# Output projection: the first eight blocks kept without x, which a chain of steps turns and adds beside the slabs

## The chip, the cores and the metric

The kernel runs on one core of a Trainium2 chip. The metric is the device time of one execution in microseconds (us), lower is better. Engines: TensorE (PE; PEld is its weight load), VectorE (DVE), ScalarE (ACT), GpSimd (POOL), SyncE (SP). DMAs are issued by instructions in the queues of SP, ACT and POOL, and an engine's queue runs in the order that was fixed when the program was built.

## The reference, cut to what matters

One layer of a decoder: 256 prompt tokens and 32 sample tokens (8 sequences of 4), D = 2048, 16 experts of which each token takes two.

```
sh1, sc1, ga1, sh2, sc2, ga2 = _adaln(c, w_ada, b_ada)
h = _rmsnorm(x, n1) * (1.0 + sc1) + sh1
...                                    # input projection, attention, gated recurrence: a, m
mix = jnp.concatenate([a, m], axis=-1) @ w_out
x = x + ga1 * mix
h2 = _rmsnorm(x, n2) * (1.0 + sc2) + sh2
x = x + ga2 * _hier_moe(h2, w_rg, b_rg, w_re, b_re, w_gate, w_up, w_down)
```

The change is in `x = x + ga1 * mix` and in the start of the second norm and of the router's logits.

## The kernel before

**Program order and the order on the engines.** The text is traced in program order; the framework then plans an order for each engine, by data dependences, by its own estimate of durations, and by program order as priority among what it holds ready. `split` (the division of a float32 tile into a rounded high part and a rest) is raised in priority. The order is fixed at build time; on the chip each engine works through its own.

**The output projection.** `out_proj` makes 32 slabs, each 512 KB of `w_out`. A slab is fetched on the ACT queue into one of three `ring0` slots (`load`, L210), split (`wh` on ACT, L495; `wl` on DVE, L496; two buffers of each), and multiplied: 24 matmuls `pf` of 128x288. Four slabs accumulate two blocks of 128 output features in two PSUM banks, and four banks (`acc`) are in use in turn, so slab n of one group of four can start only when the group before the last has had its banks emptied. Features come out transposed: a block is 128 features by 288 tokens. The order of the slabs is 0, 1, 2, 4, 5, 6, 3, 7 and then 8 to 31; below they are numbered by their place in that order, 0 to 31. Place 6 ends blocks 0 and 1, place 7 blocks 2 and 3, place 11 blocks 4 and 5, place 15 blocks 6 and 7, and so on.

**What is done with a block.** `mixed(kc, p)` empties block kc from PSUM: x (held transposed in `xT`) plus gate times product, by DVE (L1431 for the prompt, L1433 and L1434 for the samples); then the scaled copy `hA` (ACT, L1435), `hAs` (DVE), `hAb` (POOL, L1438), squares (ACT, L1440 and L1441, two buffers `sq`) and their sum `sqs` (POOL, L1443). Every fourth block turns `hA` back into rows (`pt`) and makes the router's logits (`plg`).

**The residual.** After place 6 of the slabs, the pools of the recurrence are closed and `residual` runs: four loads of `x_prompt` (512 KB each, L1464) and four of `x_sample` (64 KB each, L340) on the ACT queue into five of the seven slots of a new ring, `ring3`, which takes the closed pools' memory, and waits for the last users of it; 36 transposes `pxt` of x on PE, and nine copies into `xT`; a row shift `dsh` (matmuls `pga`) and the router's shift (`router_shift`, matmuls `prs`). Only then, in program order, comes `mixed(0)`.

**What runs beside it.** `ada` yields the steps of the modulation's matmuls: a step takes two 512 KB loads of `w_ada` (SP queue, seven slots) and makes 16 records `pm` on PE. Eight steps are woven into the last 25 slabs (`weave((out, 25), some(mods, M4))`). The experts' weights are prefetched on SP into `ring3` and `ring0`; after the projection come the second norm, the router and the experts. `tick`, called after each slab, takes the next step of a chain in `aside`; what such a step puts on PE is queued behind the slab's last matmul.

Of the kernel before, what the change touches and what calls it, by code (L numbers as in the profile page):

```python
# [10 lines left out]
F32 = mybir.dt.float32  # L11
# [3 lines left out]
AF = mybir.ActivationFunctionType  # L15
OP = mybir.AluOpType
# [4 lines left out]
KC = 16  # L21
# [96 lines left out]
def weave(*streams):  # L118

    live = [[g, n, 0] for g, n in streams if n]  # L120
    while live:
        s = min(live, key=lambda x: x[2] / x[1])
        try:
            next(s[0])
            s[2] += 1
        except StopIteration:
            live.remove(s)


class Step:  # L130
# [1287 lines left out]
        return self.run([jobs[i] for i in (0, 1, 2, 4, 5, 6, 3, 7)] + jobs[8:])  # L1418

    def mixed(self, kc, p):  # L1420
        nc = self.nc
        ga, A = self.mt[2], self.mt[4]
        cb, k = kc // 4, kc % 4
        if k == 0:
            self.hA = self.de.tile([128, 4, 256], F32, tag="hA", name="hA", bufs=2)
            self.hAs = self.de.tile([128, 4, 32], F32, tag="hAs", name="hAs", bufs=2)
            self.hAb = self.de.tile([128, 4, 128], F32, tag="hAb", name="hAb", bufs=2)
        by_seq = lambda a: a.rearrange("p (b t) -> p b t", t=4)
        bc = lambda m: m[:, kc, 1:9][:, :, None].to_broadcast([128, 8, 4])
        x, xq = self.xT[:, kc, 0:256], self.xT[:, kc, 256:288]  # L1430
        nc.vector.scalar_tensor_tensor(x, p[:, 0:256], ga[:, kc, 0:1], x, op0=OP.mult, op1=OP.add)  # L1431
        t = self.de.tile([128, 32], F32, tag="gts", name="gts", bufs=2)
        nc.vector.tensor_mul(by_seq(t), by_seq(p[:, 256:288]), bc(ga))  # L1433
        nc.vector.tensor_add(xq, xq, t)  # L1434
        nc.scalar.activation(self.hA[:, k, :], x, AF.Copy, scale=A[:, kc, 0:1])  # L1435
        nc.vector.tensor_mul(by_seq(self.hAs[:, k, :]), by_seq(xq), bc(A))
        four = lambda a: a[:, None, :].to_broadcast([128, 4, 32])
        nc.gpsimd.tensor_copy(self.hAb[:, k, :].rearrange("p (r t) -> p r t", r=4), four(self.hAs[:, k, :]))  # L1438
        sq = self.de.tile([128, 384], F32, tag="sq", name="sq2", bufs=2) if kc else self.sqs
        nc.scalar.activation(sq[:, 0:256], x, AF.Square)  # L1440
        nc.scalar.activation(sq[:, 256:384].rearrange("p (r t) -> p r t", r=4), four(xq), AF.Square)  # L1441
        if 0 < kc < KC - 1:
            nc.gpsimd.tensor_add(self.sqs, self.sqs, sq)  # L1443
        self.sql = sq
        if k == 3:
            for i in range(2):
                q = self.misc("pt2")
                for j in range(4):
                    self.tr(q[:, j * 128:(j + 1) * 128], self.hA[:, j, i * 128:(i + 1) * 128])
                self.copy(self.hs(i, cb), q)  # L1450
            q = self.misc("pt2")
            self.tr(q[:, 0:128], self.hAs.rearrange("p k t -> p (k t)"))
            self.copy(self.hs(2, cb), q[:, 0:128])
            self.logits(cb)

    def residual(self, ring):

        nc, io = self.nc, self.io
        self.xT = self.de.tile([128, KC, NT], F32, tag="xT", name="xT")
        slabs = []  # L1460
        for i in range(2):
            for h in range(2):
                t = ring[0].tile([128, 1024], F32, tag=ring[1], name="xin")
                nc.scalar.dma_start(t, io["x_prompt"][0, i * 128:(i + 1) * 128, h * 1024:(h + 1) * 1024])  # L1464
                slabs.append((i, h, t))
        t = ring[0].tile([128, 512], F32, tag=ring[1], name="xin")
        self.x_in(t.rearrange("p (k c) -> p k c", k=4), 2)
        for i, h, s in slabs:
            for q in range(2):
                p = self.misc("pxt")  # L1470
                for k in range(4):
                    self.tr(p[:, k * 128:(k + 1) * 128], s[:, (q * 4 + k) * 128:(q * 4 + k + 1) * 128])
                k0 = h * 8 + q * 4
                self.copy(self.xT[:, k0:k0 + 4, i * 128:(i + 1) * 128], p.rearrange("p (k t) -> p k t", k=4))
        p = self.misc("pxt")
        for k in range(4):
            self.tr(p[:, k * 128:(k + 1) * 128], t[:, k * 128:(k + 1) * 128])
        self.copy(self.xT[:, :, 256:288].rearrange("p (k j) t -> p k j t", j=4), p.rearrange("p (k j t) -> p k j t", k=4, j=4))

        sel = self.de.tile([128, 4, 32], F32, name="sel")  # L1480
        nc.vector.tensor_sub(sel, self.c("selb").rearrange("p (k t) -> p k t", k=4),
                             self.ident[:, 0:128:32][:, :, None].to_broadcast([128, 4, 32]))
        self.dsh = self.de.tile([128, 512], F32, name="dsh")
        p = self.misc("pga")
        for k in range(4):
            for j in range(4):
                q, c0 = self.mrow_at(k, j)
                self.mm(p[32 * j:32 * j + 32, k * 128:(k + 1) * 128], sel[:, q, :], self.mrow[3][:, c0:c0 + 128], True, True)
        self.copy(self.dsh, p)
        self.router_shift()  # L1490
        self.sqs = self.de.tile([128, 384], F32, name="sqs")
        self.lg = self.de.tile([128, 3, 20], F32, name="lg")
        self.h2 = self.mix.tile([128, 4608], F32, tag="mixT", name="h2")

    def by_rows(self):

# [15 lines left out]
    def router_shift(self):  # L1512

        p = self.misc("prs")
        for kc in range(KC):
            self.mm(p[0:9, 0:20], self.mt[3][:, kc, :], self.wr[:, kc, :], kc == 0, kc == KC - 1)
        b = self.de.tile([9, 20], F32, name="rs9")
        self.nc.vector.tensor_copy(b, p[0:9, 0:20])
        selb = self.c("selb", 9).rearrange("p (j t) -> p j t", j=4)
        p = self.misc("prs")  # L1520
        self.mm(p[:, 0:20], self.ident[0:9, 0:1].to_broadcast([9, 128]), b, True, True)
        for j in range(4):
            self.mm(p[32 * j:32 * j + 32, 32:52], selb[:, 0, :], b, True, True)
        self.rb = self.de.tile([128, 2, 20], F32, name="rb")
        for i in range(2):
            self.nc.vector.tensor_add(self.rb[:, i, :], p[:, 32 * i:32 * i + 20], self.br)

    def logits(self, cb):

        nc = self.nc  # L1530
        pl = self.misc("plg")
        for i in range(3):
            for k in range(4):
                l = self.hA[:, k, i * 128:(i + 1) * 128] if i < 2 else self.hAb[:, k, :]
                self.mm(pl[:, i * 20:(i + 1) * 20], l, self.wr[:, cb * 4 + k, :], k == 0, k == 3)
        lg = self.lg.rearrange("p i e -> p (i e)")
        if cb == 0:
            nc.vector.tensor_copy(lg, pl[:, 0:60])
        else:
            nc.vector.tensor_add(lg, lg, pl[:, 0:60])  # L1540
# [140 lines left out]
    def turned(self, sa):  # L1681
        p = self.misc("pht")
        for k in range(4):
            self.tr(p[:, k * 128:(k + 1) * 128], sa[:, k * 128:(k + 1) * 128])
        hT = self.ex.tile([128, 4, 128], F32, tag="hidT", name="hidT", bufs=2)
        self.copy(hT.rearrange("p k s -> p (k s)"), p)
        return hT
# [195 lines left out]
def body(tc, nc, io, stop=None):  # L1883
    s = Step(tc, io)
# [3 lines left out]
    def pool(name, side="left", bufs=1, space=None):  # L1888
        more = {"space": space} if space else {"side": side, "reuse_waits": "tile"}
        return tc.tile_pool(name=name, bufs=bufs, **more)  # L1890

    def some(gen, n):
        return islice(gen, n), n

    with pool("const") as const, pool("ring0", bufs=R0) as r0, pool("ring1", bufs=R1) as r1, \
# [48 lines left out]
        with pool("keep") as s.keep, pool("hga") as s.hga, pool("cc") as s.cc:  # L1944
# [8 lines left out]
            with pool("hg") as s.hg:  # L1953
# [4 lines left out]
                out = s.out_proj()  # L1958
# [9 lines left out]
        with pool("de") as s.de, pool("ring3", bufs=R3) as r3:  # L1968
            s.residual((r3, "w3"))
            weave((out, 25), some(mods, M4))  # L1970
            s.use("out", exp=[(r3, "w3")] * R3 + [r0] * R0)
            s.fetching, s.ahead = s.fetches(), []
            s.look_ahead(R3 + R0)
            held.close()
            with pool("ex", "right") as s.ex:
                s.norm2()
                s.route()
                for _ in mods:
                    pass
                s.use("experts", exp=[r1] * R1 + [r2] * R2 + [(r3, "w3")] * R3 + [r0] * R0)  # L1980
                s.once = [(s.ex, "x")] * 4 if XR else []
                s.look_ahead(R3 + len(rings) + len(s.once))
                s.experts()
# [24 lines left out]
```

## Time and profile before

| | |
|---|---|
| time, median of 3 runs | 1470.29 us (1467.14 to 1472.81) |
| the profiled execution's time | 1465.81 us |
| its span (first to last instruction) | 1463.9 us |
| PE busy | 1356.1 us (93%) |
| DMA | 457.25 MB, mean 312 GB/s |
| output projection's last 25 slabs, residual included | about 772 to 892 us of the span |

Times in rows are us from the span's start. In a timeline a row is: start, duration, engine, line, operation, out<-in, shape, count, and in brackets the idle time before it with what ended it. ACTq, SPq are DMA issues in the queues of ACT and SP. The matmuls overlap, so a run of n of them takes less than n times the duration of one.

### The profile page before, as it was taken

To read this page: it belongs to the slowest core of one execution; us is meant where nothing else is said; L and a number is where in the kernel's file an instruction comes from. 1 tells how busy PE (TensorE), PEld (TensorE's weight loads), DVE (VectorE), ACT (ScalarE), POOL (GpSimd) and SP (SyncE) were. 2 spreads that over 40 slices of the span, in tenths; PEclk is the share of its full clock that TensorE was granted. 3 is DMA by queue.
4 is the path that set the end of the run, shared out by engine and by line. 5 is a ranking of instruction groups with operands and counts; after the bars stand their busy time and mean duration, and the time that the engine had idled before them with its cause. 6 is when DMAs were issued, how large, how long until landed. Compare 5 with 4: busy or idle time off the path is not lost. (4 is left out here: it accounts for less than half of the span.)

```text
span 1463.9 us, 30058 instructions
## 1 busy us (share of the span) xinstructions
PE 1356.1 (93%) x11808; PEld 925.8 (63%) x11808; DVE 650.9 (44%) x1571; ACT 368.3 (25%) x687; POOL 145.7 (10%) x178
## 2 busy tenths in 40 slices
PE   4889899989999997999998999999999999699997
PEld 3566677777888885788775997563535445253532
DVE  2332355565885454796453444123234141413134
ACT  3222233455443353343332442010000000000000
POOL 2000201010001010012011222001010010101011
PEclk9999999999999998999998998899999999799999
DMA  9999998648889987889979646769999999799997
GB/s 314 368 382 328 354 339 306 232 152 264 287 268 290 287 271 236 274 268 309 329 235 345 243 159 238 297 268 366 399 389 396 395 388 398 269 398 387 398 387 283
DMA packets 240807, 457.25 MB, mean 312 GB/s; under 512 B 17178, under 2 KB 84619, under 8 KB 240395
## 3 DMA queue, kind: packets, MB, share of 16 engines
q1 hardware_dynamic: 171218, 374.60, 71.1%
q10 hardware_dynamic: 66818, 74.10, 15.1%
q0 software_dynamic: 2624, 6.56, 1.3%
q8 instruction: 95, 1.56, 0.4%
q14 instruction: 52, 0.43, 0.1%
HBM read 446.94 MB, written 8.26 MB: 311 GB/s over the span
## 5 line engine op out<-in xcount | busy, mean ns | idle before, releaser
L496 DVE TENSOR_TENSOR wl<-w,wh 128x1024 fp32r<-128x1024 f32 x128 | 159.5, 1246 | 164.2 <-ACT wh L495 159.8
L148 PE MATMUL pf<-hhi,wh 128*128 128x288 f32 x640 | 200.4, 313 | 1.7 <-ACT lf L788 1.4
L495 ACT CAST wh<-w 128x1024 fp32r<-128x1024 f32 x128 | 133.9, 1046 | 269.4 <-PE pf L148 199.8
L148 PE MATMUL pf<-hlo,wh 128*128 128x288 f32 x640 | 193.9, 303 | 0.0
L148 PE MATMUL pf<-hhi,wl 128*128 128x288 f32 x640 | 193.5, 302 | 0.0
L148 PE MATMUL pm<-w,cT 128*32 128x128 f32 (+1 forms) x2048 | 126.7, 361 | 26.9 <-DMA w<-w_ada 26.2
L148 PEld LDWEIGHTS pf<-hhi,wh 128*128 128x128 f32 x640 | 122.2, 191 | 17.6 <-issue 14.2
L148 PE MATMUL pa<-w,hp 128*64 128x512 f32 x512 | 118.3, 618 | 8.1 <-DMA w<-w_exp_up 8.1
L148 PEld LDWEIGHTS pf<-hlo,wh 128*128 128x128 f32 x640 | 122.6, 192 | 4.1 <-issue 3.8
L148 PEld LDWEIGHTS pf<-hhi,wl 128*128 128x128 f32 x640 | 122.5, 191 | 2.1 <-issue 1.9
L148 PE MATMUL pu<-w,hp 128*64 128x512 f32 x512 | 116.1, 594 | 0.5 <-DMA w<-w_exp_up 0.5
L148 PE MATMUL py<-w,hidT 128*64 128x512 f32 x512 | 114.6, 602 | 0.8 <-DVE hidT L196 0.8
L148 PEld LDWEIGHTS pm<-w,cT 128*32 128x32 f32 x2048 | 61.8, 118 | 71.0 <-DMA w<-w_ada 35.9
L148 PEld LDWEIGHTS pg<-oh,h 128*128 128x128 f32 x768 | 89.4, 196 | 6.5 <-issue 6.5
L148 PE MATMUL pg<-oh,h 128*128 128x128 f32 x768 | 91.5, 281 | 0.0
L148 PEld LDWEIGHTS pa<-w,hp 128*64 128x64 f32 x512 | 37.1, 143 | 80.5 <-issue 74.4
L1402 POOL TENSOR_TENSOR x<-x,gt 128x512 f32<-128x512 f32 x24 | 33.2, 1382 | 524.0 <-DVE gt L1400 521.6
L148 PEld LDWEIGHTS pu<-w,hp 128*64 128x64 f32 x512 | 37.9, 137 | 74.6 <-issue 68.4
L1679 DVE SCALAR_TENSOR_TENSOR sa<-sa,cs,pu 128x512 f32<-128x512 f32 x8 | 6.0, 747 | 172.8 <-PE pu L148 172.8
L148 PEld LDWEIGHTS py<-w,hidT 128*64 128x64 f32 x512 | 36.9, 138 | 72.0 <-issue 64.3
L148 PE MATMUL pf<-mhi,wh 128*128 128x288 f32 x256 | 77.5, 304 | 0.2 <-ACT mhi L495 0.2
L148 PE MATMUL pf<-mlo,wh 128*128 128x288 f32 x256 | 76.9, 301 | 0.0
(427 smaller groups left out, 2004.2 us busy)
## 6 DMA issues: line engine op xcount, KB each, us to landing
w<-w_ada SPq DMA_DIRECT2D x192, 512.0 KB, 7.2
w<-w_exp_gate SPq DMA_DIRECT2D x128, 512.0 KB, 10.6
w<-w_exp_up SPq DMA_DIRECT2D x128, 512.0 KB, 9.7
w<-w_exp_down SPq DMA_DIRECT2D x128, 512.0 KB, 10.5
w<-w_in ACTq DMA_DIRECT2D x96, 512.0 KB, 5.4
w<-cache_k SPq DMA_DIRECT2D x128, 256.0 KB, 4.3
w<-cache_v SPq DMA_DIRECT2D x128, 256.0 KB, 4.4
w<-w_out ACTq DMA_DIRECT2D x32, 512.0 KB, 3.6
```

Source lines behind the costliest of these rows:

```text
L148: return self.queued(self.nc.tensor.matmul(out, lhsT=lhsT, rhs=rhs, start=start, stop=stop))
L495: self.nc.scalar.copy(hi, x)
L496: self.nc.vector.tensor_sub(lo, x, hi.bitcast(F32))
L1402: eng.tensor_add(x, x, t[:, 0:n])
L1679: self.nc.vector.scalar_tensor_tensor(sa, sa, cs, pu, op0=OP.mult, op1=OP.mult)
```

## The change

For the first eight blocks `mixed` no longer reads x: ACT writes gate times product of the prompt into `xT`, and DVE that of the samples. `residual` still issues the loads of x at the same place (in the order of column halves), but all the rest of it becomes a chain, `joined`, whose steps are taken one after each slab from place 7 on: `sel`, `dsh`, the router's shift in two steps, then x for blocks 0 to 3 (transposed on PE, added to `xT` by DVE from PSUM), `scaled(0..3)`, x for blocks 8 to 15 (copied into `xT` as before), the rows and logits of blocks 0 to 3 (`block(0)`, in two steps), x for blocks 4 to 7 with `scaled(4..7)`, and `block(1)`. The blocks from 8 on are added to x as before, and `block(2)` becomes a chain too. In the diff, the unchanged middle of `scaled`, the bodies of `block` and the new signature of `logits` are left out, as are the chain's first four steps (`sel`; `pga` and `dsh`; the router's shift in two).

```diff
@@ mixed @@
-        cb, k = kc // 4, kc % 4
+        x, xq = self.xT[:, kc, 0:256], self.xT[:, kc, 256:288]
+        if kc < 8:
+            nc.scalar.activation(x, p[:, 0:256], AF.Copy, scale=ga[:, kc, 0:1])
+            nc.vector.tensor_mul(by_seq(xq), by_seq(p[:, 256:288]), gs)
+            return
+        nc.vector.scalar_tensor_tensor(x, p[:, 0:256], ga[:, kc, 0:1], x, op0=OP.mult, op1=OP.add)
+        t = self.de.tile([128, 32], F32, tag="gts", name="gts", bufs=2)
+        nc.vector.tensor_mul(by_seq(t), by_seq(p[:, 256:288]), gs)
+        nc.vector.tensor_add(xq, xq, t)
+        self.scaled(kc)
+        if kc % 4 == 3:
+            steps = self.block(kc // 4)
+            if kc < KC - 1:
+                self.aside[0].append(steps)
+            else:
+                for _ in steps:
+                    pass
+
+    def scaled(self, kc):
...
+    def block(self, cb):
+        hA, hAs, hAb = self.hA, self.hAs, self.hAb
...
+        yield
+        self.logits(cb, hA, hAb)
 
     def residual(self, ring):
...
-        for i in range(2):
-            for h in range(2):
+        for h in range(2):
+            for i in range(2):
                 t = ring[0].tile([128, 1024], F32, tag=ring[1], name="xin")
                 nc.scalar.dma_start(t, io["x_prompt"][0, i * 128:(i + 1) * 128, h * 1024:(h + 1) * 1024])
                 slabs.append((i, h, t))
         t = ring[0].tile([128, 512], F32, tag=ring[1], name="xin")
         self.x_in(t.rearrange("p (k c) -> p k c", k=4), 2)
...
+        self.aside[0].append(self.joined(slabs, t))
+
+    def joined(self, slabs, sample):
+        nc = self.nc
+        plus = lambda out, p: nc.vector.tensor_add(out, out, p)
+        def turned(i, h, s, q):
+            p = self.misc("pxt")
+            for k in range(4):
+                self.tr(p[:, k * 128:(k + 1) * 128], s[:, (q * 4 + k) * 128:(q * 4 + k + 1) * 128])
+            k0 = h * 8 + q * 4
+            (self.copy if h else plus)(self.xT[:, k0:k0 + 4, i * 128:(i + 1) * 128], p.rearrange("p (k t) -> p k t", k=4))
+        def sampled(*ks):
...
+        yield
...
+        for x in slabs[0:2]:
+            turned(*x, 0)
+        sampled(0)
+        yield
+        for k in range(4):
+            self.scaled(k)
+        yield
+        turned(*slabs[2], 0)
+        turned(*slabs[3], 0)
+        yield
+        turned(*slabs[2], 1)
+        turned(*slabs[3], 1)
+        sampled(2, 3)
+        yield
+        yield from self.block(0)
+        yield
+        for x in slabs[0:2]:
+            turned(*x, 1)
+        sampled(1)
+        for k in range(4, 8):
+            self.scaled(k)
+        yield
+        yield from self.block(1)
@@ body @@
             s.residual((r3, "w3"))
             weave((out, 25), some(mods, M4))
+            s.finish_aside()
```

## Rows read from the trace of the kernel before

**Rows 1.** Busy time of each engine in four stretches: from the cast of the slab at place 9 to the first matmul of place 8, then two stretches of the projection, and one of the experts. Columns: stretch, length, busy us and instructions of PE, PEld, DVE, ACT and POOL, granted clock, DMA share, GB/s.

```profile
776.00:800.20 24.20, 17.31 (x198) 10.00 (x197) 6.00 (x13) 4.64 (x9) 0.14 (x1) 0.79 0.95 351
808.00:840.00 32.00, 32.00 (x247) 31.87 (x246) 15.83 (x27) 13.95 (x23) 7.79 (x8) 1.00 0.65 226
840.00:892.00 52.00, 52.00 (x409) 50.14 (x409) 24.62 (x45) 20.85 (x35) 12.16 (x14) 1.00 0.57 189
988.00:1100.00 112.00, 107.89 (x641) 47.51 (x636) 35.59 (x63) 5.88 (x10) 8.34 (x6) 0.98 1.03 385
```

**Rows 2.** The same view for two stretches of 5 us inside the first of them.

```profile
780.00:785.00 5.00, 1.62 (x10) 0.55 (x10) 0.00 (x0) 0.00 (x0) 0.00 (x0) 0.62 1.03 417
790.00:795.00 5.00, 4.75 (x34) 2.61 (x38) 0.69 (x1) 1.66 (x3) 0.00 (x0) 0.66 0.89 275
```

**Rows 3.** Groups of PE's matmuls by operation from 776 to 800.2 us: count | busy us, mean ns of one | idle before them and what ended it.

```profile
L148 PE MATMUL pm<-w,cT 128*32 128x256 f32 x96 | 9.6, 463 | 4.4 <-DMA w<-w_ada 4.2
L152 PE MATMUL pxt<-cst,xin 128*128 128x128 f32 x36 | 6.3, 329 | 2.5 <-DMA xin<-x_prompt 2.1 <-DMA xin<-x_sample 0.5
```

**Rows 4.** Timeline of PE and DVE from 767 us to the first matmul of place 8 at 800.17.

```profile
766.97 1.93 PE L148 MATMUL pm<-w,cT 128*32 128x256 f32 x32
...
783.38 1.92 PE L148 MATMUL pm<-w,cT 128*32 128x256 f32 x10 [4.21 <-DMA w<-w_ada]
...
790.25 1.10 PE L152 MATMUL pxt<-cst,xin 128*128 128x128 f32 x8 [2.09 <-DMA xin<-x_prompt]
...
795.84 1.09 PE L152 MATMUL pxt<-cst,xin 128*128 128x128 f32 x8
...
797.74 0.47 DVE L1431 SCALAR_TENSOR_TENSOR xT<-pf,mt,xT 128x256 f32<-128x256 f32 x1
...
798.38 1.08 PE L148 MATMUL pga<-mrow,sel 128*32 128x128 f32 x32
...
799.28 0.96 PE L148 MATMUL prs<-wr,mt 128*9 128x20 f32 x32
...
800.17 0.40 PE L148 MATMUL pf<-mhi,wh 128*128 128x288 f32 x1
```

**Rows 5.** Timeline of the stores of the recurrent state on POOL, and of ACT and its DMA issues around the loads of x; one row of DVE (the split's second half).

```profile
774.25 1.49 POOL L1068 DMA_DIRECT2D new_state_sample<-st  x2 [3.58 <-DVE st L1064]
...
776.00 1.05 ACT L495 CAST wh<-w 128x1024 fp32r<-128x1024 f32 x1 [5.45 <-PE pf L148]
776.01 0.35 ACTq L1464 DMA_DIRECT2D xin<-x_prompt  x1
...
777.08 1.23 DVE L496 TENSOR_TENSOR wl<-w,wh 128x1024 fp32r<-128x1024 f32 x1 [3.38 <-ACT wh L495]
...
781.90 1.36 ACTq L1464 DMA_DIRECT2D xin<-x_prompt  x3
784.21 0.60 ACTq L340 DMA_DIRECT2D xin<-x_sample  x1
790.22 1.88 ACTq L340 DMA_DIRECT2D xin<-x_sample  x3
...
792.14 1.07 ACT L194 COPY xT<-pxt 128x512 f32<-128x512 f32 x2 [15.09 <-DMA xin<-x_prompt]
...
794.25 0.39 ACTq L210 DMA_DIRECT2D w<-w_out  x1
```

**Rows 6.** DMA issues from 775 to 800 us: tile, queue, count, KB each, median us from issue to landing.

```profile
xin<-x_prompt ACTq DMA_DIRECT2D x4, 512.0 KB, 10.4
...
new_state_sample<-st POOLq DMA_DIRECT2D x2, 256.0 KB, 6.4
w<-w_out ACTq DMA_DIRECT2D x1, 512.0 KB, 5.4
```

**Rows 7.** Waits of SP's DMA queue from 740 to 960 us: the waiting issue <- what it waited for: us in total, times, longest.

```profile
SPq L210 <- DMA xin<-x_prompt: 10.1, 2, 7.5
```

**Rows 8.** Timeline of ACT: the casts of `w_out` after the gap; the first two of 22.

```profile
808.00 1.05 ACT L495 CAST wh<-w 128x1024 fp32r<-128x1024 f32 x1 [3.56 <-PE pf L148]
...
811.19 1.05 ACT L495 CAST wh<-w 128x1024 fp32r<-128x1024 f32 x1 [2.15 <-PE pf L148]
```

**Rows 9.** Instructions on the tile `xT`: count, duration in ns (minimum, median, maximum), first and last start.

```profile
L1431 DVE SCALAR_TENSOR_TENSOR xT<-pf,mt,xT x16: 474/480/486, 797.7 to 891.9; 128x256 f32<-128x256 f32 x16
L1435 ACT ACTIVATE hA<-xT,mt x16: 492/500/512, 798.7 to 892.4; 128x256 f32<-128x256 f32 x16
...
L196 DVE COPY xT<-pxt x5: 681/691/692, 786.4 to 798.5; 128x512 f32<-128x512 f32 x5
```

**Rows 10.** Timeline of POOL in the projection: the same two operations alone, and beside DVE's splits.

```profile
800.06 0.29 POOL L1438 COPY hAb<-hAs 128x128 f32<-128x128 f32 x1 [24.32 <-DVE hAs L1436]
...
801.31 1.00 POOL L1443 TENSOR_TENSOR sqs<-sqs,sq 128x384 f32<-128x384 f32 x1 [0.17 <-ACT sq L1441]
...
819.94 1.78 POOL L1443 TENSOR_TENSOR sqs<-sqs,sq 128x384 f32<-128x384 f32 x1 [1.15 <-ACT sq L1441]
822.07 1.23 POOL L1438 COPY hAb<-hAs 128x128 f32<-128x128 f32 x1 [0.34 <-DVE hAs L1436]
```

**Rows 11.** Timeline of SP's DMA queue after the gap.

```profile
797.06 7.07 SPq L1718 DMA_DIRECT2D w<-w_exp_gate  x7
805.02 66.61 SPq L210 DMA_DIRECT2D w<-w_ada  x5
```

More of the change, by code (lines that the diff above doesn't have):

```diff
@@ L1421, in mixed @@
         nc = self.nc
-        ga, A = self.mt[2], self.mt[4]
-        cb, k = kc // 4, kc % 4
+        ga = self.mt[2]
+        by_seq = lambda a: a.rearrange("p (b t) -> p b t", t=4)
+        gs = ga[:, kc, 1:9][:, :, None].to_broadcast([128, 8, 4])
+        x, xq = self.xT[:, kc, 0:256], self.xT[:, kc, 256:288]
[17 more added lines that the diff above has]
+        nc = self.nc
+        A = self.mt[4]
+        k = kc % 4
         if k == 0:
@@ L1428, in mixed @@
         by_seq = lambda a: a.rearrange("p (b t) -> p b t", t=4)
-        bc = lambda m: m[:, kc, 1:9][:, :, None].to_broadcast([128, 8, 4])
         x, xq = self.xT[:, kc, 0:256], self.xT[:, kc, 256:288]
[L1431 to L1434, printed above, removed]
         nc.scalar.activation(self.hA[:, k, :], x, AF.Copy, scale=A[:, kc, 0:1])
-        nc.vector.tensor_mul(by_seq(self.hAs[:, k, :]), by_seq(xq), bc(A))
+        nc.vector.tensor_mul(by_seq(self.hAs[:, k, :]), by_seq(xq), A[:, kc, 1:9][:, :, None].to_broadcast([128, 8, 4]))
         four = lambda a: a[:, None, :].to_broadcast([128, 4, 32])
@@ L1444, in mixed @@
         self.sql = sq
-        if k == 3:
-            for i in range(2):
[L1447 to L1450, printed above, removed]
-            q = self.misc("pt2")
-            self.tr(q[:, 0:128], self.hAs.rearrange("p k t -> p (k t)"))
-            self.copy(self.hs(2, cb), q[:, 0:128])
-            self.logits(cb)
+    def block(self, cb):
+        hA, hAs, hAb = self.hA, self.hAs, self.hAb
+        for i in range(2):
+            q = self.misc("pt2")
+            for j in range(4):
+                self.tr(q[:, j * 128:(j + 1) * 128], hA[:, j, i * 128:(i + 1) * 128])
+            self.copy(self.hs(i, cb), q)
+        q = self.misc("pt2")
+        self.tr(q[:, 0:128], hAs.rearrange("p k t -> p (k t)"))
+        self.copy(self.hs(2, cb), q[:, 0:128])
+        yield
+        self.logits(cb, hA, hAb)
     def residual(self, ring):
@@ L1460, in residual @@
         slabs = []
-        for i in range(2):
-            for h in range(2):
+        for h in range(2):
+            for i in range(2):
                 t = ring[0].tile([128, 1024], F32, tag=ring[1], name="xin")
@@ L1467, in residual @@
         self.x_in(t.rearrange("p (k c) -> p k c", k=4), 2)
[L1468 to L1478, printed above, removed]
+        self.sqs = self.de.tile([128, 384], F32, name="sqs")
+        self.lg = self.de.tile([128, 3, 20], F32, name="lg")
+        self.h2 = self.mix.tile([128, 4608], F32, tag="mixT", name="h2")
+        self.aside[0].append(self.joined(slabs, t))
+    def joined(self, slabs, sample):
+        nc = self.nc
+        plus = lambda out, p: nc.vector.tensor_add(out, out, p)
[6 more added lines that the diff above has]
+        def sampled(*ks):
+            p = self.misc("pxt")
+            for k in ks:
+                self.tr(p[:, k * 128:(k + 1) * 128], sample[:, k * 128:(k + 1) * 128])
+                (plus if k < 2 else self.copy)(self.xT[:, 4 * k:4 * k + 4, 256:288],
+                                               p[:, k * 128:(k + 1) * 128].rearrange("p (j t) -> p j t", j=4))
+        yield
         sel = self.de.tile([128, 4, 32], F32, name="sel")
@@ L1489, in residual @@
         self.copy(self.dsh, p)
[L1490 to L1493, printed above, removed]
+        yield
+        yield from self.router_shift()
+        yield
[12 more added lines that the diff above has]
+        sampled(2, 3)
+        yield
+        yield from self.block(0)
+        yield
+        for x in slabs[0:2]:
[3 more added lines that the diff above has]
+            self.scaled(k)
+        yield
+        yield from self.block(1)
     def by_rows(self):
@@ L1518, in router_shift @@
         self.nc.vector.tensor_copy(b, p[0:9, 0:20])
+        yield
         selb = self.c("selb", 9).rearrange("p (j t) -> p j t", j=4)
@@ L1526, in router_shift, with logits @@
             self.nc.vector.tensor_add(self.rb[:, i, :], p[:, 32 * i:32 * i + 20], self.br)
-    def logits(self, cb):
+    def logits(self, cb, hA, hAb):
         nc = self.nc
@@ L1533, in logits @@
             for k in range(4):
-                l = self.hA[:, k, i * 128:(i + 1) * 128] if i < 2 else self.hAb[:, k, :]
+                l = hA[:, k, i * 128:(i + 1) * 128] if i < 2 else hAb[:, k, :]
                 self.mm(pl[:, i * 20:(i + 1) * 20], l, self.wr[:, cb * 4 + k, :], k == 0, k == 3)
```

## The prediction

> **What bounds the kernel now.** I read the busy time by stretches first [rows 1]. In the experts DMA is full (1.03, 385 GB/s) with PE at 96%, and from 808 to 892 us PE is busy without a gap while DMA stands at 0.57 to 0.65. Between 776.0 and 800.2 it is otherwise: PE is busy 17.3 of 24.2 us, and part of that at a granted clock of 0.62 to 0.66, a mean over the two levels of 1.2 and 2.4 GHz, after waits of several us [rows 2]. So this stretch holds lost PE time, and what follows it is PE-bound until 892. The experts begin from whatever time that leaves: their loads are paced by slots that PE frees, and DMA had room before. A gain there should reach the end whole.
>
> What PE needed there I make from the groups [rows 3] and from what the same work takes in runs at full clock [rows 4]: 96 records of `pm` at 1.93/32 = 0.060 us, 5.8; 36 transposes at 1.09/8 = 0.136, 4.9; `pga` 1.1; `prs` 1.0. Together 12.8 of 24.2 us, so 11.4 us are lost.
>
> Why PE waits: place 8 starts at 800.17, behind the first emptying of a block, DVE's 797.74 [rows 4]. Its split had long been made; what lacks is a bank, since `mixed(0)` adds to an x that is only being loaded and turned. And x is late for two reasons. The second to fourth loads of `x_prompt` are issued at 781.90, about when the last stores of the state land (774.25 plus 6.4) [rows 5, 6], whose memory `ring3` takes over; three of the `x_sample` loads only at 790.22 [rows 5]. The code gives the last ones no reason, but SP's issues of `w_ada` too are held by landings of x [rows 7], so an issue can wait for an earlier DMA of the other queue. While ACT's queue holds an issue, the engine holds everything behind it: there is no ACT work between 777.05 and 792.1 and no `w_out` load before 794.25 [rows 5].
>
> **The change part by part.**
>
> *Emptying without x.* Blocks 0 to 3 need only their products and the gate. ACT takes about 0.5 us for a 128x256 with a scale, DVE 0.48 for what it replaces [rows 9]. Blocks 0 and 1 are complete before place 7, so they should be emptied before the x loads become ready, and place 8 should follow place 7 at about 776 or one `pm` step (16 records, 0.96) later. ACT's added 8 x 0.5 us lie in 116 us where it is busy 40% [rows 1]: nothing on the path.
>
> *The chain.* PE gets the same 36 transposes, `pga`, `prs`, `pt` and `plg`, only later, between slabs; the 12.8 us are moved, not saved. DVE adds 128x512 from PSUM where DVE or ACT copied: no row shows that add; bounded by the copy, 0.69, and by twice that [rows 9]; I take 0.7. Four such adds, 3 to 6 us, lie in DVE's idle half [rows 1].
>
> *What stays.* The eight x issues stand at the same place in ACT's queue, with the same waits. So the cast for place 10, ready when place 8 is done, can be caught behind them. A slab costs 3.19 us (808.00 to 811.19) [rows 8]. PE from 776.0: one `pm` step, places 8 and 9, `pga`: 1.0 + 6.4 + 1.1, to 784.5. ACT: the three x loads end at 783.3, the sample's four take 0.6 each [rows 5]. If they are held only by the first x load (784.2), they end at 786.6, and cast and `wl` take 2.3 more (776.00 to 778.31) [rows 5]: place 10 at 788.9, a stall of 4.4. If the planner puts the cast ahead of them, 785.6, a stall of 1.1. I take 3. If they are held until 790.22 as now, ACT is free at 792.1 and place 10 starts at 794.4: a stall of 10.
>
> *The next in line* is the `w_out` slab of place 12, issued behind x at about 786.6. Its landing: 5.4 us as now, or 10.4 as x's in the full queue [rows 6], so 792 to 797, plus 2.3. PE reaches place 12 after places 10 and 11 (6.4), a `pm` step and `prs` (2.0), from 787.5: at 795.9. The stall is 0 to 3.4; I take 1. DMA has less to do there than before: `pm` steps are no longer run in a row, and their slots ask for `w_ada` later.
>
> *The sum.* 11.4 lost now; 3 + 1 lost after; gain 7.4 us. The profiled execution of 1465.81 (span 1463.9) would become 1458.4. It stands 4.5 us under the median of the runs shown, 1470.29, from which I take the same 7.4: 1462.9. A measurement of this kernel tells about 0.5%, 7.4 us, so the forecast stands on that line.
>
> Costs that I put at nothing: five `ring3` slots stay with x until place 18 instead of 798, so up to five expert loads move back by some 40 us; DMA at 0.57 to 0.65 hides them [rows 1]; without that cover they would be 5 x 0.5 MB at 385 GB/s, 6.8 us. [...]
>
> **The rivals.**
>
> *All of the stall goes.* If the emptying, the cast and the load for place 12 all come ahead of the x loads in the planned order, or the waits fall differently, nothing is left in the stretch: 11.4 us, 1458.9. For it: the cast of place 9 came ahead of the x loads, though its text stands behind them [rows 5]. Against it: place 10's cast is ready 3 to 4 us later, and the x issues then are not yet through.
>
> *The stall moves from x's landing to x's issue.* ACT is held until 792.1: 11.4 - 10 = 1.4 us of gain, 1468.9. For it: the issues at 790.22 as they are [rows 5]. Against it: the hold goes by which DMAs were issued between, and five of the `w_ada` loads around them should move away with their `pm` steps. The Trainium skill, "DMA: Bandwidth & Descriptors", section "Anatomy of one DMA", says that a DMA's semaphore wait happens on the issuing sequencer before dispatch; this trace agrees, with 15 us without ACT work.
>
> *Bursts of `scaled`.* Four blocks' `scaled` come in one step, twice. POOL takes 0.29 + 1.00 for a block alone, 1.23 + 1.78 beside other work [rows 10], 3.0 against ACT's 1.2. With two `sq` buffers ACT's third square would wait for POOL's sum, and a cast stand behind it. Of each burst two squares wait 1.8 us, and so do those that pile up: 4 to 11 us of ACT in all, of which the 0.9 us of slack in a slab of 3.19 (2.3 used) covers a part. The gain shrinks to 4, or to a loss of 3.6: 1466 to 1474. Against it: casts are raised in priority, ACT and POOL are mostly idle, and pairs of blocks stretched in the same way cost PE nothing from 808 on [rows 1, 10]. The Trainium skill, "SBUF — State Buffer", section "Who interferes with whom", states as a rule that a DVE instruction with two SBUF inputs contends with a GpSimd one that reads SBUF; the split's second half is such an instruction, and the stretched 1.23 and 1.78 agree.
>
> *Slower: SP's queue.* The expert loads for slots that x holds could stand in SP's order ahead of `w_ada` loads, as seven of them do now [rows 11]. The slots come free after place 18, at about 797 + 7 x 3.2 = 819; the seven `w_ada` slots hold three and a half steps, so that from the fifth step, about place 16 to 19 (810), PE would wait until 819 plus a landing of about 7: some 16 us. Then 1462.9 + 16 = 1479. It decides as soon as one such load stands ahead of the fifth step's; the planner takes what it holds ready first, which speaks against it.
>
> **How the numbers follow.** Forecast (gain 5 to 9.5 us, 1460.8 to 1465.3) 0.43; all of the stall gone (1458 to 1460.8) 0.20; the stall moved (1465.3 to 1470) 0.19; bursts (1466 to 1474) 0.10; SP's queue (1477 to 1481) 0.08. Under 1462.9 lie the second case and a bit more than half of the first: faster 0.45. Over 1477.6 lie most of the last and a little for what I do not see: slower 0.10. The same 0.45. The range leaves out most of the last two and a little below: 1457 to 1470.5; the forecast's own is 1460.8 to 1465.3.
>
> **What the profile after would show.** Right: `pf` of place 8 at 776 to 778, not 800; ACT's scaled copies ahead of the x issues; a first PE gap near 784 that a cast ends, not DMA x; a second, if any, ended by `w_out`; `pxt` from about 800 on, between slabs, without gaps; the projection's last `pf` and everything behind it 5 to 10 us earlier, with the experts' stretch as long as now. Wrong would be: the x issues held until 792 with PE idle from 784; casts idle for `sq`; SP holding an expert load before a late `w_ada`; or an earlier end of the projection that the experts take back.

## The result, and the profile after

The changed kernel takes 1459.92 us (median of 12 runs, 1457.46 to 1468.62) against 1469.47 (12 runs, 1463.48 to 1474.22) for the kernel before. The medians are 9.6 us apart; the ratio taken over the runs is 0.9946, with a 95% interval of 0.9925 to 0.9968, and by it the change is worth 8 us, 5 to 11 by the interval. The forecast was 1462.9. The profiled execution took 1457.83 us, with a span of 1455.8.

First the busy time of each engine by stretches of the kernel after, from the end of place 7 to the end of the projection (columns as in [rows 1]):

```profile
771.00:788.20 17.20, 17.20 (x194) 15.35 (x193) 4.54 (x6) 3.43 (x4) 0.00 (x0) 1.00 1.01 372
788.20:803.00 14.80, 11.77 (x97) 9.99 (x98) 6.12 (x14) 5.91 (x10) 0.94 (x4) 1.00 0.85 286
803.00:835.00 32.00, 30.98 (x256) 29.00 (x255) 16.51 (x31) 17.06 (x39) 9.76 (x14) 1.00 0.73 247
835.00:843.00 8.00, 8.00 (x55) 8.00 (x54) 1.35 (x2) 2.14 (x5) 2.35 (x3) 0.79 0.60 200
843.00:882.00 39.00, 39.00 (x322) 36.89 (x321) 16.32 (x31) 14.60 (x26) 8.06 (x9) 1.00 0.65 213
```

Where PE was busy 17.31 of 24.2 us, with a granted clock of 0.79 [rows 1], it now works 17.2 us without a gap at 1.00, and DMA is as full as it was. The gap is not gone: 3.0 us of it are found in 788.2 to 803. PE's timeline says at which matmuls:

```profile
770.94 1.07 PE L148 MATMUL pm<-w,cT 128*32 128x256 f32 x16
771.94 0.40 PE L148 MATMUL pf<-mhi,wh 128*128 128x288 f32 x1
...
791.09 0.40 PE L148 MATMUL pf<-mhi,wh 128*128 128x288 f32 x1 [1.42 <-ACT wh L495]
...
800.37 0.40 PE L148 MATMUL pf<-mhi,wh 128*128 128x288 f32 x1 [0.89 <-ACT wh L495]
...
801.63 0.40 PE L148 MATMUL pf<-mhi,wl 128*128 128x288 f32 x1 [0.72 <-DVE wl L496]
```

Place 8 starts at 771.94, one `pm` step after place 7, where it stood 24 us behind it [rows 4]. Places 9 to 11 follow without a gap. The gaps that are left stand at places 12 and 14, and both wait for a cast. ACT's timeline tells why the casts are late (under it, three of its DMA issues by themselves):

```profile
760.98 0.83 ACT L1428 ACTIVATE xT<-pf,mt 128x256 f32<-128x256 f32 x2
...
771.06 0.35 ACTq L1488 DMA_DIRECT2D xin<-x_prompt  x1
771.87 0.47 ACT L1428 ACTIVATE xT<-pf,mt 128x256 f32<-128x256 f32 x1
776.27 0.35 ACTq L1488 DMA_DIRECT2D xin<-x_prompt  x1
776.66 1.05 ACT L495 CAST wh<-w 128x1024 fp32r<-128x1024 f32 x1 [4.33 <-DMA new_state_sample<-st]
776.84 0.82 ACTq L1488 DMA_DIRECT2D xin<-x_prompt  x2
778.51 1.05 ACT L495 CAST wh<-w 128x1024 fp32r<-128x1024 f32 x1 [0.80 <-PE pf L148]
778.52 5.08 ACTq L340 DMA_DIRECT2D xin<-x_sample  x4
784.91 3.75 ACTq L210 DMA_DIRECT2D w<-w_out  x2
788.71 0.47 ACT L1428 ACTIVATE xT<-pf,mt 128x256 f32<-128x256 f32 x1 [9.15 <-DMA w<-w_out]
789.99 1.04 ACT L495 CAST wh<-w 128x1024 fp32r<-128x1024 f32 x1 [0.81 <-DMA w<-w_out]
...
799.27 1.04 ACT L495 CAST wh<-w 128x1024 fp32r<-128x1024 f32 x1 [4.37 <-DMA w<-w_out]
```

```profile
783.03 0.57 ACTq L340 DMA_DIRECT2D xin<-x_sample  x1
784.91 0.40 ACTq L210 DMA_DIRECT2D w<-w_out  x1
788.27 0.39 ACTq L210 DMA_DIRECT2D w<-w_out  x1
```

Blocks 0 and 1 are emptied at 760.98, ahead of every load of x. The cast for place 10 (776.66) was planned between the second and the third x load, and the one for place 11 ahead of the `x_sample` loads. Then ACT's queue is held at DMA issues. A row of several issues spans the waits between them: of the 5.08 us of `x_sample` the issues themselves are 2.9 (2.48 before: 0.60 and 1.88 [rows 5]), and ahead of the fourth, at 783.03, the queue waits 2.1 us. It waits 1.3 us more before `w_out` for place 12 goes out at 784.91, and 3.0 us before the next `w_out`, at 788.27. From place 12 on the casts wait for `w_out` to land.

The trace tells what these issues wait for: each waits for a semaphore (a counter that a landing DMA raises), and an earlier DMA carries the same one. The fourth `x_sample` load shares its semaphore with the second `x_prompt` load, which lands at 783.00; `w_out` for place 12 shares one with the third `x_prompt` load, which lands at 784.89. In all four profiles of the changed kernel these two are the same, and this `w_out` is issued 0.02 us after that landing.

SP's queue shows what else the full DMA carries in that time:

```profile
762.59 9.88 SPq L210 DMA_DIRECT2D w<-w_ada  x6
775.01 3.68 SPq L1782 DMA_DIRECT2D w<-w_exp_gate  x2
787.64 5.18 SPq L210 DMA_DIRECT2D w<-w_ada  x4
```

Two loads of the experts' weights, the first of which stood at 797.06 before [rows 11], are issued at 775 and 778, into the two slots of `ring3` that x leaves free.

**How much of the 8 us is the change.** Each kernel has four profiled executions. The table cuts the span in four. PE idle is length less busy time in one window over the stretch from the end of place 7 to the projection's last matmul; lost to clock is half of PE's busy time in those spells of the stretch in which the granted clock was 0.50.

| profile | time | place 7 ends | stretch behind it | of it PE idle | lost to clock | norm, router | experts |
|---|---|---|---|---|---|---|---|
| before, 1 | 1465.81 | 776.1 | 115.8 | 6.9 | 4.0 | 41.2 | 530.8 |
| before, 2 | 1468.64 | 779.4 | 115.4 | 6.8 | 3.4 | 41.1 | 530.9 |
| before, 3 | 1470.0 | 777.0 | 118.0 | 8.2 | 5.0 | 41.3 | 531.8 |
| before, 4 | 1471.96 | 782.0 | 117.2 | 8.3 | 3.9 | 39.7 | 531.0 |
| **mean** | 1469.1 | 778.6 | 116.6 | 7.5 | 4.1 | 40.8 | 531.1 |
| after, 1 | 1457.83 | 771.0 | 111.0 | 4.1 | 1.7 | 39.4 | 534.4 |
| after, 2 | 1460.12 | 773.8 | 112.4 | 4.6 | 2.6 | 41.2 | 530.9 |
| after, 3 | 1466.04 | 781.8 | 110.5 | 2.4 | 3.4 | 39.3 | 531.9 |
| after, 4 | 1462.9 | 776.5 | 109.0 | 2.4 | 1.7 | 43.9 | 531.8 |
| **mean** | 1461.7 | 775.8 | 110.7 | 3.4 | 2.3 | 41.0 | 532.3 |

The stretch of the change is 5.9 us shorter: 4.2 less idle and 1.7 less lost to the clock. Length less both losses is 105 us within 0.3 in every row: the work is the same. Of the 7.4 us between the means, 2.9 come from ahead of place 7's end and 1.2 are given back behind the stretch; both are smaller than the spread between profiles of one kernel. PE's instructions ahead of there are the same; ACT and DVE empty blocks 0 to 2 in the last 10 us of it, but in the first pair of profiles the kernels are 5.1 us apart before that (the same DVE row at 754.65 and at 749.56).

### The profile page after: what moved, and what is told of

It reads as the page before. It is cut to its first block, busy times and chain, and to the rows that moved or that the text cites. A ratio compares the mean times of both kernels' runs of the same rounds, so it can differ in the third digit from the quotient of the medians.

```text
span 1455.8 us, 30060 instructions
## 1 busy us (share of the span) xinstructions
PE 1351.4 (93%) x11808; PEld 923.0 (63%) x11808; DVE 645.6 (44%) x1559; ACT 370.0 (25%) x694; POOL 142.9 (10%) x178
## 5 line engine op out<-in xcount | busy, mean ns | idle before, releaser
L148 PE MATMUL pm<-w,cT 128*32 128x128 f32 (+1 forms) x2048 | 122.2, 355 | 19.6 <-DMA w<-w_ada 19.1
L148 PEld LDWEIGHTS pf<-hhi,wh 128*128 128x128 f32 x640 | 121.3, 190 | 17.2 <-issue 13.8
L148 PE MATMUL pf<-mhi,wl 128*128 128x288 f32 x256 | 76.8, 300 | 0.7 <-DVE wl L496 0.7
## 6 DMA issues: line engine op xcount, KB each, us to landing
w<-w_exp_gate SPq DMA_DIRECT2D x128, 512.0 KB, 10.5
w<-w_exp_down SPq DMA_DIRECT2D x128, 512.0 KB, 10.5
```

The source lines that it names most:

```text
L148: return self.queued(self.nc.tensor.matmul(out, lhsT=lhsT, rhs=rhs, start=start, stop=stop))
```

## The experiments

**The two kernels again.** First beside the experiments below:

> The kernel before, profiled once more. In the two profiles at hand the first matmul of place 7 starts at 771.8 (before) and 766.7 us (after), though all that runs up to there is the same program; the stretch from the end of place 7 to the end of the projection's last slab matmul takes 115.8 and 111.0 us. Theory (the 5.1 us ahead of the change are chance, the change's own part is the stretch): the stretch is again 115.8 within 0.7, and the start of place 7 lies anywhere from 765 to 774. Rival (the 5.1 us belong to the change, by its code's place or size): the start is again 771.8 within 1 us.

> The changed kernel, profiled once more. Theory: the stretch from the end of place 7 to the last slab matmul is again 111.0 us within 0.7, with a first gap of 1 to 2 us at place 12 that a late w_out load ends, and the start of place 7 lies anywhere from 765 to 774. Rival (the time ahead belongs to the change): it starts at 766.7 within 1 us.

> The kernel before, profiled a third time. Theory (ahead of place 7 is chance, the change's own part in the projection is about 4 us): the stretch from the end of place 7 to the last slab matmul is again 115.4 to 115.8 us, gaps of 10 to 11.5 us in it; the start of place 7 anywhere from 765 to 777. Rival (the kernel before is slower ahead of place 7 for a reason of its own): the start lies later than 771 again, and later than in the changed kernels of this call.

Then, since the changed kernel had been early ahead of place 7 already in both of its profiles:

> A further look at the changed kernel as it is. Three looks at the kernel before ended place 7 at 776.1, 779.4 and 777.0 us, two at the changed one at 771.0 and 773.8, though no engine's instructions differ ahead of there. If that is chance, place 7 ends anywhere from 771 to 779 here; if the change moves it, at 771 to 774. The stretch from there to the projection's last matmul: 111 to 112.5 us if the two looks so far are typical, and any difference between looks is made of spells at the lower clock and of the gap at place 12.

> The same again, on the same terms: place 7 ends at 771 to 774 if the change moves it, anywhere from 771 to 779 if it is chance; the stretch behind it 110 to 113 us.

> A fourth look at the kernel before, on the same chip as these: place 7 ends at 776 to 780 if the two kernels differ ahead of there, anywhere from 771 to 779 if it is chance; the stretch behind it 115 to 118 us, about 4.5 more than the changed kernel's.

Measured: the table above. Place 7 of the changed kernel ended at 781.8 and 776.5 in its last two profiles, of the kernel before at 782.0: the ranges lie over each other, 771 to 782 and 776 to 782. The five variants below, which are the same up to there but for one wait, ended it at 772.0 to 777.9. So the 5 us by which the first profile was ahead there can't be told from chance, and the first pair of profiles alone would have told a wrong story, a gain of 8 us of which the change's own stretch held 4.8. The stretch, 109.0 to 112.4 against 115.4 to 118.0, doesn't overlap. It spreads more than was expected: of the six repeats two, the first and the last of the kernel before, fall where the stretch was put; 112.4, 110.5 and 109.0 of the changed kernel and 118.0 of the kernel before miss by 0.5 to 2.2 us. The ends of place 7 at 781.8 and 782.0 lie outside what either theory gave, 771 to 780.

**Undone: blocks 0 and 1 wait for x, all else as changed.** The emptying gets a bias that is x times zero, from the last `x_prompt` load.

```diff
-            nc.scalar.activation(x, p[:, 0:256], AF.Copy, scale=ga[:, kc, 0:1])
+            if kc < 2:
+                nc.scalar.activation(x, p[:, 0:256], AF.Identity, bias=self.zero, scale=ga[:, kc, 0:1])
+            else:
+                nc.scalar.activation(x, p[:, 0:256], AF.Copy, scale=ga[:, kc, 0:1])
@@ residual, behind the loads @@
+        self.zero = self.de.tile([128, 1], F32, name="zero")
+        nc.gpsimd.tensor_scalar(self.zero, slabs[3][2][:, 0:1], 0.0, None, op0=OP.mult)
```

> The changed kernel, but the emptying of blocks 0 and 1 waits for the landing of the last of the four x_prompt loads (its bias is that slab's first column times zero); the chain and all its steps stay. Theory (the gain is that the banks are emptied before x is there): place 8 starts at about 788 to 792 instead of 772, minus what pm and pga can fill, the stretch grows by 9 to 14 us to 120 to 125, and the kernel is no faster than before: ratio 0.998 to 1.005. Rival (the gain is that the transposes and the rest are spread between slabs): the ratio stays at 0.995 and the stretch at 111.

Measured: 1474.16 us, ratio 1.0039 (1.0018 to 1.0061), as expected; the stretch is 126.2 us, 1.2 above the range given (in a profiled execution of 1478.41 us). ACT's timeline, and under it the first matmul of place 8 in PE's:

```profile
784.60 1.36 ACTq L1491 DMA_DIRECT2D xin<-x_prompt  x3
787.08 7.55 ACTq L340 DMA_DIRECT2D xin<-x_sample  x4
798.70 0.56 ACT L1429 ACTIVATE xT<-pf,zero,mt 128x256 f32<-128x256 f32 x1 [19.73 <-DMA xin<-x_sample]
```

```profile
799.54 0.61 PE L148 MATMUL pf<-mhi,wh 128*128 128x288 f32 x1 [2.50 <-DVE xT L1432]
```

With the wait for x back, place 8 is back at 799.54, 21.9 us behind place 7 (17 to 21 were expected), with ACT idle for 19.7 us behind the issues of x. The whole gain hangs on the emptying that doesn't wait for x; the chain by itself gains nothing, nor does the new order of the x loads or ACT in DVE's place, which this variant keeps. That the stretch is 9.6 us longer than the mean before fits the order: the turning of x, which filled 4.9 us of the gap before, now comes after it. PE is idle for 13.9 us of the stretch against 7.5, and loses 8.3 us to the lower clock against 4.1.

**Expert loads held back, 1.** No load of the experts' weights is issued before the last `w_ada` load.

```diff
+        d = getattr(self.nc, QUEUE[kind]).dma_start(dst, src)
+        if kind == "ada":
+            self.last_ada = d.ins
@@ body @@
-            s.look_ahead(R3 + R0)
+            with tc.issue_after(s.last_ada):
+                s.look_ahead(R3 + R0)
```

> The changed kernel, but the first ten expert loads stand on SP behind the last w_ada load of the projection; in the changed kernel two of them (1 MB) are issued at 775 and 778 us, ahead of the w_out loads that PE then waits for at places 12 to 14 (3.5 us in three gaps). Theory A (those gaps are a full DMA): the two loads are 2.6 us at 400 GB/s, the gaps shrink by 1.5 to 2.6 us and the stretch to 108.5 to 109.5. Theory B (the gaps are the late issue of w_out behind x on ACT's queue): the stretch stays at 111 within 0.5. For either: the experts start no later, since DMA has room from 846 on; if it has not, the gap shows as a wait of the first expert.

Measured: 1461.39 us, ratio 0.9952 (0.9927 to 0.9978). The busy time in two windows, SP's queue, ACT's issue of `w_out` for place 12, and PE's wait in the second window:

```profile
777.70:802.00 24.30, 24.16 (x255) 20.73 (x255) 7.29 (x12) 6.34 (x8) 0.00 (x0) 1.00 1.01 344
840.00:860.00 20.00, 17.93 (x134) 16.88 (x133) 6.79 (x13) 5.87 (x11) 3.39 (x5) 0.91 0.96 343
```

```profile
834.82 7.97 SPq L1784 DMA_DIRECT2D w<-w_exp_gate  x7
```

```profile
789.21 2.75 ACTq L210 DMA_DIRECT2D w<-w_out  x2
```

```profile
850.15 0.40 PE L148 MATMUL pf<-mhi,wh 128*128 128x288 f32 x1 [1.34 <-ACT wh L497]
```

The gaps at places 12 and 14 are gone: so the two early expert loads made them. How they did can be read from the issues. `w_out` for place 12 now shares its semaphore with a `w_ada` load issued 10 us before, and goes out 11.5 us behind place 7 (at 789.21), as soon as the `x_sample` issues are through; in the changed kernel it is 13.9 to 15.9. It isn't that DMA has room: the third `x_prompt` load lands 13.8 us behind place 7, against 13.9 to 15.9, and from its issue to its cast `w_out` takes 6.4 us, against 4.8 to 6.1.

But now seven expert loads go out in a row at 834.82, DMA is full there, and the casts wait for `w_out` at place 23: PE idles 2.1 us in that window, 2.6 in the stretch. Here the landing itself is late: that `w_out`, issued at 839.02, is cast at 849.05. The stretch is 109.9 us, between the 108.5 to 109.5 of the one theory and the 110.5 to 111.5 of the other.

**Expert loads held back, 2.** The same, but they may go from an earlier `w_ada` load on (`ada_loads` lists these in order), so that they don't come in one row.

```diff
-            s.look_ahead(R3 + R0)
+            with tc.issue_after(s.ada_loads[171]):
+                s.look_ahead(R3 + R0)
```

> The changed kernel, but its ten first expert loads stand on SP behind one earlier w_ada load (that of the sixth of the eight steps, issued at about 792 in the changed kernel), so that the two that were issued at 775 and 778 follow the w_out loads of places 12 to 14, and the others stay spread. Theory A (the left-over gaps are the full DMA): no gap at places 12 to 14 and none near 850, where seven expert loads in a row delayed w_out when they were all held to 835; gaps of 1 to 2 us in all, stretch 107.5 to 109; the kernel 2 to 4 us faster than the changed one, ratio 0.990 to 0.994. Rival (what the projection gains is taken back by the router's stretch and the experts): stretch as said, but a ratio of 0.995 and a first expert matmul that starts no earlier after the residual's place than in the changed kernel.

Measured: 1460.82 us, ratio 0.9940 (0.9918 to 0.9961). ACT's timeline, and two windows:

```profile
786.19 2.62 ACTq L342 DMA_DIRECT2D xin<-x_sample  x4
788.86 1.86 ACTq L210 DMA_DIRECT2D w<-w_out  x2
...
794.82 1.04 ACT L497 CAST wh<-w 128x1024 fp32r<-128x1024 f32 x1 [0.95 <-DMA w<-w_out]
```

```profile
777.80:803.00 25.20, 25.20 (x265) 22.10 (x266) 9.57 (x15) 8.02 (x11) 0.00 (x0) 1.00 1.04 354
...
825.80:829.80 4.00, 4.00 (x21) 4.00 (x20) 1.06 (x1) 0.00 (x0) 0.00 (x0) 0.57 0.48 162
```

PE has no gap in 25.2 us behind place 7 (777.8), though DMA is still full, 1.04. What has changed is the time in ACT's queue: `x_sample` goes out in 2.62 us without a wait (5.1 to 5.8, waits included, in the four profiles of the changed kernel), `w_out` for place 12 is issued 11.1 us behind place 7 (13.9 to 15.9 there) and its cast runs 17.0 us behind it (19.0 to 22.0), 6.0 us after the issue. As in the variant before, its semaphore is that of a `w_ada` load and not of the third `x_prompt` load. PE's idle time in the stretch is 1.5 us against 3.4. By its runs the kernel is not told apart from the changed one, where 2 to 4 us were expected: two spells of lower clock, one of them in the window at 0.57, cost 3.4 us of the stretch, which takes 109.3 (107.5 to 109 expected).

**x loads put off.** The `x_sample` loads are issued in the chain's third step, the second halves of `x_prompt` in its fourth, to bring `w_out` for place 12 forward.

```diff
-                nc.scalar.dma_start(t, io["x_prompt"][0, i * 128:(i + 1) * 128, h * 1024:(h + 1) * 1024])
+                if h == 0:
+                    self.load_x(i, h, t)
...
-        self.x_in(t.rearrange("p (k c) -> p k c", k=4), 2)
@@ joined @@
+        self.x_in(sample.rearrange("p (k c) -> p k c", k=4), 2)
...
+        for x in slabs[2:4]:
+            self.load_x(*x)
```

> The changed kernel, but the sample's loads are issued with the chain's third step and the two x_prompt loads of the second column half with its fourth; w_out of place 12 then stands ahead of 1 MB of x on ACT's queue, w_out of place 13 behind it. The two early expert loads stay. Theory A (full DMA): as 1 MB less stands ahead of it, w_out of place 12 lands 2 to 3 us earlier and its gap of 1.5 to 3.5 us goes, that of places 13 and 14 stays or grows to 2 or 3: stretch 109 to 111, ratio 0.993 to 0.996. Theory B (issue order alone): all gaps at places 12 to 14 go, stretch 107 to 108.

Measured: 1465.91 us, ratio 0.9949 (0.9925 to 0.9973); its runs spread from 1455.5 to 1467.9, so that median and ratio don't say quite the same. ACT's timeline and PE's:

```profile
787.56 0.60 ACTq L210 DMA_DIRECT2D w<-w_out  x1
788.20 1.00 ACTq L1482 DMA_DIRECT2D xin<-x_prompt  x2
791.95 1.05 ACT L495 CAST wh<-w 128x1024 fp32r<-128x1024 f32 x1 [3.98 <-DMA w<-w_out]
791.97 0.42 ACTq L210 DMA_DIRECT2D w<-w_out  x1
...
803.26 1.04 ACT L495 CAST wh<-w 128x1024 fp32r<-128x1024 f32 x1 [7.42 <-DMA w<-w_out]
```

```profile
804.35 0.61 PE L148 MATMUL pf<-mhi,wh 128*128 128x288 f32 x1 [4.15 <-ACT wh L495]
```

`w_out` for place 12 is issued 9.7 us behind place 7, its cast runs at 14.1, and the gap there is gone. It stands at place 13 instead, with 4.15 us: that slab's load is issued behind the two put off loads of x and is cast 11.3 us after its issue. The stretch is 114.1 us, 3.4 longer than the changed kernel's mean; neither theory, 109 to 111 and 107 to 108, had that. In this stretch a load that is moved past another only hands on the wait.

**The chain in one tick.** All steps behind the router's shift are taken at place 16 at once: eight blocks' transposes, adds, `scaled` and logits.

```diff
-            yield
+            for _ in range(5):
+                yield
@@ joined: the yields behind it are taken out @@
-        yield from self.block(0)
+        for _ in self.block(0):
+            pass
```

> The changed kernel, but all of the chain that touches x (36 transposes, the adds and copies, scaled of eight blocks, the rows and logits of blocks 0 to 7) is traced after one slab, place 16, instead of in nine steps after places 12 to 20; the planner may still spread it behind that slab. Theory (spreading is worth little, the emptying is all): the stretch is 110 to 113, at most 2 us more than the changed kernel's. Rival (bursts): ACT's squares wait for POOL's sums and casts stand behind them; casts late by 4 to 11 us in all, stretch 115 to 120, no faster than before.

Measured: 1466.34 us, ratio 0.9979 (0.9957 to 1.0001). Three windows:

```profile
788.00:798.00 10.00, 6.92 (x52) 4.93 (x51) 1.69 (x5) 1.89 (x3) 0.00 (x0) 0.75 1.00 312
...
805.00:828.00 23.00, 23.00 (x183) 21.29 (x182) 11.37 (x19) 12.37 (x25) 4.78 (x7) 1.00 0.68 230
...
828.00:848.00 20.00, 20.00 (x138) 18.48 (x139) 9.98 (x21) 8.72 (x23) 8.59 (x12) 0.83 0.53 182
```

Where the burst runs, 805 to 848, PE has no gap at all, and full clock until 828: the bursts of `scaled` leave PE no wait. The stretch is nevertheless 115.9 us, outside the 110 to 113 of the theory and at the length that the rival gave, but without the rival's waits. It holds the gap at place 12, 3.1 us, ahead of the one tick, with a clock of 0.75 around it, much as in the second profile of the changed kernel (3.4 us); and from 828 to 848 a clock of 0.83, 3.4 us. Whether the one tick has a part in these, or this profile had them by chance, is open: by runs the intervals of this kernel and the changed one still meet (0.9957 and 0.9968).

## Why the prediction was right, and where its steps were not

**The size.** 1462.9 was forecast and 1459.92 measured, from a gain of 7.4. By the four profiles on each side the stretch gained 5.9, inside the 5 to 9.5 given for this case. The time itself is below this case's own 1460.8 to 1465.3 and in the range of "all of the stall goes", which did not happen. That is luck as far as the profiles show it: the gain was taken off 1470.29 where the 12 runs have 1469.47, and what the runs gained beyond 5.9, which their interval doesn't tell from 5.9, has no place in the stretch.

**Lost before, 11.4.** Right: 7.5 idle and 4.1 at the lower clock, 11.6 in the mean. After, the sum had 4 and the profiles have 5.7: 3.4 idle and 2.3 at the lower clock.

**Emptying without x.** Right, and what the gain hangs on: place 8 followed one `pm` step behind place 7, and undoing it gave the gap back. The costs of what the trace of before could not show, from the rows on `xT` after:

```profile
L1428 ACT ACTIVATE xT<-pf,mt x8: 466/472/489, 761.0 to 811.8; 128x256 f32<-128x256 f32 x8
...
L1501 DVE TENSOR_TENSOR xT<-xT,pxt x6: 280/678/686, 796.1 to 827.9; 128x512 f32<-128x512 f32 x4, 128x128 f32<-128x128 f32 x2
```

0.47 us for ACT's scaled copy (0.5 taken), 0.68 for DVE's add of 128x512 from PSUM (0.7 taken).

**The cast for place 10, a stall of 3.** Wrong in place. The planner put it between the x loads, nearer to the lower of the two ends (1.1), and it was held 4.3 us by the issue ahead of it only while PE worked on places 8 and 9: no gap in three profiles, 0.7 us in the second. The Trainium skill, "DMA: Bandwidth & Descriptors", section "Anatomy of one DMA — SWDGE (gpsimd) path", has the semaphore wait of a DMA on the issuing sequencer. The section is on DMAs of GpSimd, these are ACT's; the cast's 4.33 us of idle time behind an `xin` issue agree.

**`w_out` for place 12, a stall of 1 (0 to 3.4).** The term that was mis-sized: 1.4, 3.4, 1.9 and 1.8 us in the four profiles, with 1.6, 0.2 and 0.3 more at places 13 and 14 in three of them. The step that failed is "issued behind x at about 786.6", 10.5 us behind place 7: it was issued 13.9 to 15.9 us behind it. The landing was not the trouble: 4.8 to 6.1 us from issue to cast, near the lower of the two values taken (5.4). The prediction knew that an issue can wait for an earlier DMA, but had that wait for the sample's loads alone, and took it to go with the `w_ada` loads that move away. They did move away; two expert loads took their place, and with them `w_out` came to share a semaphore with the third `x_prompt` load. So "DMA has less to do there than before" didn't come true either (1.01), but the two kernels that held the expert loads back show that the issue made the gap at place 12: DMA was as full (1.01 and 1.04), the way from issue to cast as long, and the gap went with the wait.

**What was put at nothing.** The sum after has no term for the lower clock, which took 2.3 us. The small gaps at transposes were not in it: 0.5 us at place 16 in one profile, 0.2 to 0.5 at place 20 in all four. The "some 40 us" by which expert loads move back do not fit the prediction's own times, 798 to 819; measured from place 7, two were issued 17 us later than the first before, three 34 us later, and two 17 and 14 us earlier. The expert loads that x pushes back cost at most 1.1 us in the experts (532.3 against 531.1), less than the spread of one kernel's profiles.

**The rivals.** The stall as a whole didn't move to the issue of x, though that issue is held: the casts for places 10 and 11 stand ahead of the `x_sample` loads. A part of it did, to the `w_out` issue behind them. Bursts of `scaled`: the squares waited as foretold, but for little, as the chain of waits of the kernel after has it (us in total, times, longest):

```profile
ACT sq L1460 <- POOL sqs L1463: 1.9, 3, 0.9
```

Against the 4 to 11 us put on it, and with the chain in one tick PE still had no gap there. SP's queue: expert loads did get ahead, but at 775, into slots that were free, not at 819 in front of a late `w_ada`; their price was a gap of 1.4 to 3.4 us, not 16. All of the stall gone: the second kernel with the expert loads held back comes nearest, and its one profile gains 1.4 us on the changed one's mean stretch, which is within that one's spread.

## What to carry to other kernels

When one wait holds a stretch, look for the instruction whose operand is late although its result doesn't need it yet: taking x out of the emptying was worth 5.9 us where no engine had less to do. What is left in a stretch with a full DMA is handed from one load to the next, so count what the freed time and the freed slots will fetch, in which queue an issue stands in front of a cast, and which earlier landing that issue waits for: two more loads in another queue moved `w_out` by 2.4 us or more. And compare a stretch over several profiles before a few microseconds are put down to a cause: here a single pair showed 5 us ahead of the change that more profiles did not keep.

## What the hardware showed beside this

The granted clock fell where PE had no idle time at all. In the third profile of the kernel before PE worked without a gap at full clock, then without a gap at the lower of its two levels:

```profile
801.30:869.40 68.10, 68.10 (x547) 67.31 (x544) 33.41 (x69) 30.45 (x56) 18.91 (x22) 1.00 0.57 198
869.40:872.90 3.50, 3.50 (x17) 3.50 (x16) 0.60 (x1) 0.00 (x0) 0.00 (x0) 0.51 0.43 149
```

The first profile after has the like at 835 to 843 us: 0.79, with PE busy 8.00 of 8.00 us, 1.7 us lost, some 6 us behind a gap of 0.54. Such a spell within the projection is found in two of four profiles of each kernel, and in two places of the kernel in one tick and of the second one that held the expert loads back; no row shows what sets it off. With [rows 1], which has 1.00 from 808 to 892, I had taken it that a PE without gaps keeps its clock there.

A DMA issue in one queue waited for the landing of an earlier DMA with the same semaphore, also where the code has no dependence between the two. Before, three `x_sample` loads stood until 790.22 in this way: the second shares its semaphore with the second `x_prompt` load, which landed at 790.20.

The same instructions took 771.0 to 781.8 us to the end of place 7 in four profiles of one kernel, and the part from the projection to the experts' first matmul took 39.3 to 43.9. A difference of 0.5% in this kernel is no more than what one profile differs from the next.
